# Two kinds of sums of a hybrid streaming encoder, moved from VectorE and GpSimd into accumulating transfers

## The chip, the cores and the metric

The kernel runs on one core of one Trainium2 chip. The metric is the device time of one execution in microseconds; of several runs the median counts. The engines are TensorE (PE in the profile, PEld for its weight loads), VectorE (DVE), ScalarE (ACT), GpSimd (POOL) and SyncE (SP). SP computes nothing here; it issues nearly all transfers, in order. A DMA issued by SP, ScalarE or GpSimd stands in that engine's own instruction stream.

## The reference

Two layers over 2048 tokens of width 1024. The first is a pooling mixer; the second, whose last part the change touches, is attention with 16 heads of 64 channels, followed by a gate, an output projection and a gated embedding:

```python
k_sh = rms_norm(split_heads(k_all), k_norm)
v_sh = split_heads(v_all)
q, z = jnp.split(rms_norm(x, b_norm[j]) @ b_w_in[j], 2, axis=-1)
q = rms_norm(split_heads(q), b_q_norm[j])
o = stick_breaking_attention(q, k_sh, v_sh)       # A[t,s] = beta[t,s] * prod_{s<j<t} (1 - beta[t,j])
x = x + (o * jax.nn.silu(z)) @ b_w_out[j]
x = x + (p[i] @ ple_w[i]) * jax.nn.sigmoid(x @ ple_gate_w[i])
```

The attention weight of key s for query t is the sigmoid of their logit times the product of (1 - sigmoid) over all keys between s and t. Keys after the query count nothing.

## The kernel before, in words

The first half of the program (to about 1333 us) computes the mixer layer and k, v and q, in four passes over 512 tokens each. It leaves x in DRAM (x2d, and x2p split into two parts for matmul), k, q and differences of neighbouring v rows (kd, qd, vd), and weights that are already split (wzd for z, wod for the output projection, wgd for the gate, wld for the embedding). Each fp32 operand of a matmul is held as a pair of fp32r tiles, a rounded part and the rest; a product is three matmuls, in the attention two.

The second half is attention. Four query chunks c of 512 tokens are done in the order 3, 2, 1, 0; in each, 16 heads; for each head the key chunks kc from c down to 0. One (chunk, head, key chunk) is four slots, and the loop over `n` does one slot a turn. In a slot:

- `front` (L924, L925): two matmuls make the logits of 128 queries by 512 keys, ScalarE makes 1 - sigmoid (L928, into one of four kap tiles), VectorE runs the product along the keys as a scan (L936; L933 on the diagonal chunk, where widths are 128 to 512).
- `turn`, six slots later: four transposes on TensorE (L949) into a psa bank (two of them), ScalarE copies it (L952) and VectorE makes the rest (L953), which frees the bank.
- `gather`, eight slots later: two matmuls (L961, L962) add at times v into pso.

When a head's last gather is done, pso holds 128 rows by 512 queries: 64 channels from v's rounded part, and the same 64 from the rest. ScalarE copies one half of the rows to `ob` (L976) and the other to `os` (L977), one and two slots later; two heads share an `os` and an `ob`, 64 rows each. When both heads of a pair are done, `os` and `ob` are added on VectorE (L979), which completes both heads' outputs, and `gated` follows: SP loads z's gate (L969), ScalarE adds a bias in four pieces (L972), GpSimd multiplies (L974). Later `pair_up` splits `os` into an og pair (L1006 ScalarE, L1007 GpSimd). What happens so many slots later is put off with `soon(k, fn)` and run by `settle`.

Between these, in each slot, TensorE gets filler matmuls: in chunk 3 the products for z's gate (`gate_z`, L1028 to L1034), in chunk 2 what is left of those and `post(3)`, in chunk 1 `post(2)`, in chunk 0 `post(1)`; `post(0)` is the tail. The tables `share` and `even` set how many filler matmuls a slot gets, with `stops` as the slots in which a chunk's outputs are complete.

`post(c)` has two phases over eight blocks o of 128 channels. First the output projection: weights wod (L212, by `stored`), x2d loaded into `xr` (L1065), 24 matmuls, VectorE adds the product to `xr` (L1068), and `halves` splits `xr` into an x3 pair (L1072 ScalarE, L1073 GpSimd). Then the gate and embedding: 24 matmuls for the gate and 6 for the embedding, a sigmoid into `sg` (L1092), VectorE multiplies (L1106), and the final sum adds both parts of x3 to `sg`: one on GpSimd (L1107), one on VectorE (L1108). SP stores `sg` to the output (L1112), one block late (`late`). The tiles `xr`, `sg`, `zr` and `sgz` share four buffers.

A scheduler orders the instructions of each engine by its own estimates, except those held with `keep_in_program_order` (`stay`, `held`); L972, L976, L977 and the casts are held so. Each engine works through its list in order, and an instruction that waits holds up all that stand behind it.

## Time and profile before

| what | us |
|---|---|
| median of 3 runs (2697.16 to 2699.16) | 2697.47 |
| the profiled execution | 2696.51 |
| its span, first to last instruction | 2694.7 |
| attention, chunk 3 (about) | 1333 to 1840 |
| attention, chunk 2 (about) | 1840 to 2190 |
| attention, chunk 1 (about) | 2190 to 2440 |
| attention, chunk 0 (about) | 2440 to 2596 |
| tail, `post(0)` | 2596 to 2695 |

In a row of groups stand the line, the engine, the operation, output and inputs, shape and count, then busy us, the mean ns of one, and the engine's idle time just before them with what ended it. A row of waits says who waited, for whom, for how long in all, how often, and the longest. A row of the timeline has the start, the duration, the engine and the instruction; SPq and ACTq are the issue of a transfer; the time in brackets is what the engine idled before it and what ended that. PEld rows are weight loads, and the load of a transpose is that of its moved tile.

### The profile page before, as it was taken

The numbers are of one execution on the slowest core, as the hardware profiler recorded it, in microseconds if no ns is written. First come the engines' busy times: TensorE is split into PE (matmuls) and PEld (weight loads), VectorE is DVE, ScalarE is ACT, GpSimd is POOL, SyncE is SP. The second block draws the span as 40 slices with busy tenths as digits, with TensorE's granted clock in tenths as the row PEclk, the third lists the DMA queues.
The fourth block names the chain that finished last, engine by engine and source line by source line (L and its number), as shares of the span: only waits on it lengthen the run. The fifth ranks groups of instructions, "written<-read, shape, count | busy, mean of one in ns | idle before, by whom it ended". The sixth has DMA issues, their size and how long they took to land. (4 is left out here: it accounts for less than half of the span.)

```text
span 2694.7 us, 38618 instructions
## 1 busy us (share of the span) xinstructions
PE 2673.6 (99%) x13352; PEld 2226.5 (83%) x13352; DVE 1941.9 (72%) x2506; ACT 1399.0 (52%) x2735; POOL 922.0 (34%) x724
## 2 busy tenths in 40 slices
PE   9999999999999999999999999999999999999999
PEld 8888888888888888888878888888888888888887
DVE  6776626755367643755399999999999998986632
ACT  6445523555135541445366666666666666665531
POOL 2675338643485434753121111122111211222220
PEclk9999999999999999999999999999999999999999
DMA  8657785567856678444788665555655576668865
GB/s 328 222 168 279 252 302 193 198 229 254 300 180 223 242 241 305 145 150 149 223 239 281 195 210 173 163 165 181 198 164 173 173 214 199 197 198 262 268 226 172
DMA packets 276688, 581.56 MB, mean 216 GB/s; under 512 B 33126, under 2 KB 67174, under 8 KB 276492
## 3 DMA queue, kind: packets, MB, share of 16 engines
q1 hardware_dynamic: 270754, 571.41, 64.5%
q10 hardware_dynamic: 5738, 7.68, 1.0%
q8 instruction: 106, 1.74, 0.3%
q14 instruction: 90, 0.74, 0.1%
HBM read 438.40 MB, written 132.19 MB: 212 GB/s over the span
## 5 line engine op out<-in xcount | busy, mean ns | idle before, releaser
L952 ACT CAST at<-psa 128x512 fp32r<-128x512 f32 (+3 forms) x640 | 334.3, 522 | 439.1 <-PE psa L949 429.4
L614 PE MATMUL psd<-wpair,x 128*128 128x512 f32 x2304 | 536.8, 391 | 0.0
L936 DVE TENSOR_TENSOR_SCAN pp<-kap,pp,zeros 128x512 f32<-128x512 f32 x384 | 513.1, 1336 | 6.1 <-ACT kap L928 5.1
L614 PEld LDWEIGHTS psd<-wpair,x 128*128 128x128 f32 x2304 | 429.8, 188 | 87.1
L953 DVE TENSOR_TENSOR at<-psa,at 128x512 fp32r<-128x512 f32 (+3 forms) x640 | 381.3, 596 | 82.0 <-ACT at L952 77.3
L949 PE MATMUL psa<-ident,pp 128*128 128x128 f32 x2176 | 344.6, 273 | 10.7 <-DVE at L953 10.3
L928 ACT ACTIVATE kap<-psl 128x512 f32<-128x512 f32 (+3 forms) x640 | 345.0, 539 | 13.2 <-PE psl L925 10.3
L949 PEld LDWEIGHTS psa<-ident,pp 128*128 128x128 f32 x2176 | 265.4, 140 | 77.7 <-DVE at L953 21.9
L924 PE MATMUL psl<-kk,qa 128*128 128x512 f32 (+3 forms) x640 | 282.3, 441 | 0.1
L962 PE MATMUL pso<-at,vv 128*128 128x512 f32 (+3 forms) x640 | 234.4, 366 | 1.3 <-DVE at L953 1.3
L925 PE MATMUL psl<-kk,qb 128*128 128x512 f32 (+3 forms) x640 | 232.9, 364 | 0.0
L961 PE MATMUL pso<-at,vv 128*128 128x512 f32 (+3 forms) x640 | 232.8, 364 | 0.1
L933 DVE TENSOR_TENSOR_SCAN pp<-kap,ahead 128x128 f32<-128x128 f32 (+3 forms) x256 | 227.0, 887 | 5.1 <-ACT kap L928 3.2
L167 PE MATMUL psd<-xp,wpair 128*128 128x512 f32 x512 | 199.5, 390 | 1.7 <-DVE xp L316 1.7
L166 PE MATMUL psd<-xp,wpair 128*128 128x512 f32 x512 | 200.0, 391 | 0.4 <-ACT xp L315 0.3
L168 PE MATMUL psd<-xp,wpair 128*128 128x512 f32 x512 | 199.3, 390 | 0.0
L149 DVE SCALAR_TENSOR_TENSOR wpair<-wraw,gains,wpair 128x512 fp32r<-128x512 f32 x192 | 161.4, 883 | 48.9 <-ACT wpair L148 48.9
L143 POOL TENSOR_TENSOR wpair<-wraw,wpair 128x512 fp32r<-128x512 f32 x99 | 144.0, 1464 | 84.2 <-ACT wpair L141 78.8
L148 ACT ACTIVATE wpair<-wraw,gains 128x512 fp32r<-128x512 f32 x192 | 132.7, 718 | 68.9 <-DMA wraw<-in_bq_dram 31.1
L1033 POOL TENSOR_TENSOR zr<-zr,sgz 128x512 f32<-128x512 f32 x32 | 62.0, 1938 | 307.1 <-ACT sgz L1032 269.2
L141 ACT CAST wpair<-wraw 128x512 fp32r<-128x512 f32 x148 | 89.9, 618 | 122.1 <-PE psd L168 98.9
L962 PEld LDWEIGHTS pso<-at,vv 128*128 128x128 f32 x640 | 120.3, 188 | 27.7 <-DVE at L953 1.7
(200 smaller groups left out, 5365.7 us busy)
## 6 DMA issues: line engine op xcount, KB each, us to landing
kk<-kd SPq DMA_DIRECT2D x320, 128.0 KB
vv<-vd SPq DMA_DIRECT2D x160, 256.0 KB
wraw<-in_kv_dram SPq DMA_DIRECT2D x128, 256.0 KB
wpair<-wzd SPq DMA_DIRECT2D x64, 512.0 KB
wpair<-wod SPq DMA_DIRECT2D x64, 512.0 KB
wpair<-wgd SPq DMA_DIRECT2D x64, 512.0 KB
wpair<-wu SPq DMA_DIRECT2D x48, 512.0 KB
wpair<-wi SPq DMA_DIRECT2D x36, 512.0 KB
```

Source lines behind the costliest of these rows:

```text
L166: T.matmul(ps, wst(units, kt, 0, c0), acts[kt][:, 0], start=(begin and kt == order[0]), stop=False)
L614: T.matmul(pss2[i], ck["x2"][kt][:, xh, tk], wst(ws, kt, wh, 0, W5), start=(kt == 0 and xh == 0 and wh == 0), stop=(kt == KT - 1 and wh == 1))
L924: T.matmul(ps[:, :w], qa[:, qs], kk[:, :w], start=True, stop=False)
L925: T.matmul(ps[:, :w], qb[:, qs], kk[:, :w], start=False, stop=True)
L928: A.activation(out=kp[:, r0:], in_=ps[:, :w], func=AF.Sigmoid, scale=-1.0)
L933: V.tensor_tensor_scan(out=pp[:, r0:][:, ::-1], data0=kp[:, r0:][:, ::-1], data1=ahead[:, r0:][:, ::-1], initial=1.0, op0=ALU.mult, op1=AL ...
L936: V.tensor_tensor_scan(out=pp[:, ::-1], data0=kp[:, ::-1], data1=zeros.to_broadcast([P, W5]), initial=st["carry"][j], op0=ALU.mult, op1=AL ...
L949: T.transpose(pt[:, j * P : (j + 1) * P], pp[:, r0 + kt * P : r0 + (kt + 1) * P], ident)
L952: A.copy(out=at[:, 0, cs], in_=pt[:, cs])
L953: V.tensor_tensor(out=at[:, 1, cs], in0=pt[:, cs], in1=f(at[:, 0, cs]), op=ALU.subtract)
L961: T.matmul(po[:, cs], vv[:, kt, :], at[:, 0, cs], start=(st["diag"] and kt == 0), stop=False)
L962: T.matmul(po[:, cs], vv[:, kt, :], at[:, 1, cs], start=False, stop=(st["last"] and kt == 3))
```

## The change

- In chunks 3, 2 and 1 the sum of two heads' outputs is no longer made by VectorE (L979) but by a transfer that GpSimd issues, from `ob` onto `os`, with addition. `gated` comes six slots after the last gather in place of four, and `os` is handed on after eight in place of six. Chunk 0 keeps the sum on VectorE.
- In `post(3)` and `post(2)`, `xr` (x after the output projection) is stored to the output by SP as soon as it is made. The two final sums (L1107, L1108) are gone there; in their place a transfer issued by GpSimd adds `sg` to what stands in the output, one block late as the store was. `post(1)` and `post(0)` keep the sums.
- The tables of filler matmuls count two slots more at a chunk's end.

```diff
@@ gather
                 if half:
-                    soon(3, lambda: V.tensor_tensor(out=os, in0=os, in1=ob, op=ALU.add))
-                    soon(4, gated)
-                    soon(6, lambda: outs[c].append(os))
+                    if c:
+                        soon(3, lambda: nc.gpsimd.dma_start(out=os, in_=ob, accum_op=ALU.add))
+                        soon(6, gated)
+                        soon(8, lambda: outs[c].append(os))
+                    else:
+                        soon(3, lambda: V.tensor_tensor(out=os, in0=os, in1=ob, op=ALU.add))
+                        soon(4, gated)
+                        soon(6, lambda: outs[c].append(os))
@@ post, first phase
                 V.tensor_tensor(out=xr, in0=ps, in1=xr, op=ALU.add)
                 pr = pair("x3")
+
+                if c > 1:
+                    nc.sync.dma_start(out=outt[o * P : (o + 1) * P, c * W5 : (c + 1) * W5], in_=xr)
@@ post, second phase
                 V.tensor_tensor(out=sg, in0=pl, in1=sg, op=ALU.mult)
-                (V if tail[0] else G).tensor_tensor(out=sg, in0=sg, in1=f(x3[o][:, 1]), op=ALU.add)
-                summed = soon(2, lambda o=o, sg=sg: V.tensor_tensor(out=sg, in0=sg, in1=f(x3[o][:, 0]), op=ALU.add))
-
-                def finish(o=o, sg=sg, summed=summed):
+                whole = outt[o * P : (o + 1) * P, c * W5 : (c + 1) * W5]
+                summed = lambda: None
+                if c < 2:
+                    (V if tail[0] else G).tensor_tensor(out=sg, in0=sg, in1=f(x3[o][:, 1]), op=ALU.add)
+                    summed = soon(2, lambda o=o, sg=sg: V.tensor_tensor(out=sg, in0=sg, in1=f(x3[o][:, 0]), op=ALU.add))
+
+                def finish(sg=sg, summed=summed, whole=whole):
                     summed()
-                    nc.sync.dma_start(out=outt[o * P : (o + 1) * P, c * W5 : (c + 1) * W5], in_=sg)
+                    if c > 1:
+                        nc.gpsimd.dma_start(out=whole, in_=sg, accum_op=ALU.add)
+                    else:
+                        nc.sync.dma_start(out=whole, in_=sg)
@@ the tables
-            stops[c] = 4 * (n + 1) + LAG_G + 6
+            stops[c] = 4 * (n + 1) + LAG_G + 8
-                        even = POST / (64.0 * c - (LAG_G + 2 if c == 1 else 1))
+                        even = POST / (64.0 * c - (LAG_G + 4 if c == 1 else 1))
```

Three places show how instructions move. Lines from 976 on have other numbers in the changed kernel: the transfer onto `os` is L980, the store of `xr` L1077, the transfer onto the output L1124; L1007, L1065 and L1073 of before are L1012, L1070 and L1081.

First ScalarE, at the second head pair of chunk 3, from the copy into `os` to the bias. Before:

```order
L977 COPY os<-pso 64x512
L952 CAST at<-psa 128x512
L928 ACTIVATE kap_12444<-psl 128x512
L952 CAST at<-psa 128x512
L928 ACTIVATE kap_12445<-psl 128x512
L972 ACTIVATE os<-os,en 128x128 x4
```

With the change:

```order
L977 COPY os<-pso 64x512
L952 CAST at<-psa 128x512
L928 ACTIVATE kap_12444<-psl 128x512
L952 CAST at<-psa 128x512
L928 ACTIVATE kap_12445<-psl 128x512
L952 CAST at<-psa 128x512
L928 ACTIVATE kap_12442<-psl 128x512
L1037 ACTIVATE sgz<-zr 128x512
L952 CAST at<-psa 128x512
L928 ACTIVATE kap_12443<-psl 128x512
L972 ACTIVATE os<-os,en 128x128 x4
```

The bias stands two slots further back: four copies and four sigmoids lie between, where there were two of each.

Second GpSimd, in chunk 2, where the second phase of `post(3)` begins. Before:

```order
L1007 TENSOR_TENSOR og<-os,og 128x512
L1107 TENSOR_TENSOR sg<-sg,x_19137 128x512
L974 TENSOR_TENSOR os<-os,zt 128x512
L1107 TENSOR_TENSOR sg<-sg,x_19313 128x512
L1007 TENSOR_TENSOR og<-os,og 128x512 x2
L1107 TENSOR_TENSOR sg<-sg,x_19509 128x512
```

With the change:

```order
L1012 TENSOR_TENSOR og<-os,og 128x512
L1124 DMA out_dram<-sg 128x512
L980 DMA os<-ob 128x512
L974 TENSOR_TENSOR os<-os,zt 128x512
L1012 TENSOR_TENSOR og<-os,og 128x512
L1124 DMA out_dram<-sg 128x512
```

The sums are gone, and issues of both kinds stand between the operations that stay.

Third SP, in the first phase of `post(3)`, with the change:

```order
L192 DMA qa<-qd_2_210 64x512 x2
L193 DMA qb<-qd_2_210 64x512
L1077 DMA out_dram<-xr 128x512
L193 DMA qb<-qd_2_210 64x512
L212 DMA wpair<-wod_275 128x1024
L1070 DMA xr<-x2d_4_132 128x512
L200 DMA kk<-kd_2_242 64x512 x2
```

And before, in its second phase, where the final sums are stored:

```order
L192 DMA qa<-qd_7_215 64x512
L193 DMA qb<-qd_7_215 64x512
L1112 DMA out_dram<-sg 128x512
L200 DMA kk<-kd_7_247 64x512 x2
L205 DMA vv<-vd_1_261 128x512
L212 DMA wpair<-wgd_286 128x1024
```

A store that waits for VectorE stands between loads of q, k, v and weights in both; it has moved from the second phase to the first.

## The prediction

> **What bounds the kernel now.** I read the page first, then the busy times of the four attention stages, then what TensorE waited for in them.
>
> ```profile
> span 2694.7 us, 38618 instructions
> PE 2673.6 (99%) x13352; PEld 2226.5 (83%) x13352; DVE 1941.9 (72%) x2506; ACT 1399.0 (52%) x2735; POOL 922.0 (34%) x724
> ```
>
> TensorE is busy for nearly the whole span. The change touches attention alone, so the share that matters is that of its stages. The next rows are the windows view: chunk 3, chunk 2, chunk 1, chunk 0, each with the busy time of PE, PEld, DVE, ACT and POOL, then clock, DMA share and GB/s.
>
> ```profile
> 1333.00:1840.00 507.00, 503.67 (x2776) 419.58 (x2776) 488.58 (x582) 324.94 (x650) 86.18 (x48) 1.00 0.66 203
> 1840.00:2190.00 350.00, 346.11 (x1919) 289.57 (x1918) 340.44 (x414) 230.72 (x476) 62.89 (x36) 1.00 0.57 178
> 2190.00:2440.00 250.00, 245.79 (x1359) 206.70 (x1358) 221.97 (x290) 158.40 (x348) 48.66 (x33) 1.00 0.69 206
> 2440.00:2596.00 156.00, 154.66 (x804) 129.84 (x803) 93.68 (x146) 81.71 (x195) 40.78 (x31) 1.00 0.83 254
> ```
>
> VectorE is as full as TensorE in chunks 3 and 2 (488.58 of 507, 340.44 of 350), less in chunk 1 (221.97 of 250), and has room in chunk 0. The change takes work from VectorE, and only what TensorE loses by waiting for VectorE can come back. The waits view says how much that is; the first two rows are of the window 1333 to 1840, the other two of 1840 to 2440 (total, times, longest).
>
> ```profile
> PEld psa L949 <- DVE at L953: 7.5, 15, 1.6
> PE psa L949 <- DVE at L953: 2.2, 4, 1.2
> ...
> PEld psa L949 <- DVE at L953: 14.4, 21, 1.5
> PE psa L949 <- DVE at L953: 8.1, 13, 1.1
> ```
>
> The two rows of a pair are one stall seen twice: the weight load of a transpose can't start until VectorE has emptied the bank, and the matmul behind it starts late. The matmul's row is too small (its predecessor is still drawn as busy), the load's too large (some of it is ordinary slack). So TensorE loses 8.1 to 14.4 us in chunks 2 and 1, and 2.2 to 7.5 in chunk 3. That is the ceiling of this change: 10.3 to 21.9 us, under 1% of the span. One stall in the timeline shows its origin:
>
> ```profile
> 2102.44 0.66 DVE L1106 TENSOR_TENSOR sg<-psd,sg 128x512 f32<-128x512 f32 x1
> 2103.23 1.30 POOL L1107 TENSOR_TENSOR sg<-sg,x 128x512 f32<-128x512 f32 x1 [3.62 <-PE pso L962]
> 2103.62 1.99 DVE L933 TENSOR_TENSOR_SCAN pp<-kap,ahead 128x512 f32<-128x512 f32 x1
> 2104.50 2.22 POOL L1007 TENSOR_TENSOR og<-os,og 128x512 fp32r<-128x512 f32 x1
> 2105.54 1.72 DVE L1108 TENSOR_TENSOR sg<-sg,x 128x512 f32<-128x512 f32 x1
> 2107.19 0.68 DVE L953 TENSOR_TENSOR at<-psa,at 128x512 fp32r<-128x512 f32 x1
> 2107.92 0.42 PEld L949 LDWEIGHTS psa<-ident,pp 128*128 128x128 f32 x4 [1.32 <-DVE at L953]
> ```
>
> The final sum has three steps: L1106, L1107 on GpSimd, L1108. GpSimd's step makes the scan wait (1.99 us), the next GpSimd operation makes L1108 wait (1.72), L953 comes late, and the transposes start 1.32 us late. So a final sum costs VectorE more than its own instruction.
>
> **The change, part by part.** First what goes. The rows are of the grouped lines, window 1333 to 1840 and then 1840 to 2440 (busy, mean ns):
>
> ```profile
> L979 DVE TENSOR_TENSOR os<-os,ob 128x512 f32<-128x512 f32 x8 | 5.3, 665 | 0.0
> ...
> L979 DVE TENSOR_TENSOR os<-os,ob 128x512 f32<-128x512 f32 x16 | 11.8, 736 | 0.0
> L1107 POOL TENSOR_TENSOR sg<-sg,x 128x512 f32<-128x512 f32 x16 | 22.6, 1414 | 86.6 <-DVE sg L1106 62.1 <-PE psl L925 20.9 <-PE pso L962 3.6
> L1108 DVE TENSOR_TENSOR sg<-sg,x 128x512 f32<-128x512 f32 x15 | 18.5, 1236 | 6.4 <-POOL sg L1107 6.4
> ```
>
> VectorE loses 5.3 us in chunk 3 (1% of its 488.58) and 11.8 + 18.5 = 30.3 in chunks 2 and 1 (5% of 562.4; the 16th final sum lies just past the window). GpSimd loses 22.6 us of operations that also block the scans. What that gives TensorE lies between 0, if the stalls stay for other reasons, and the ceiling. In chunks 2 and 1 I take three quarters of the middle of 8.1 and 14.4, so 8.5 us: the stalls cluster at the final sums, while L1007 and L1073 on GpSimd remain and still collide with scans. In chunk 3 only 1% of VectorE's work goes and no final sum; there I take 1 us of 2.2 to 7.5. Gross gain 9.5.
>
> **The wait that is added.** The four activations L972 add a bias to os, in ScalarE's fixed order, and must now wait until the accumulating transfer has landed. Behind them on ScalarE stand the copies L952, which free the transposes' banks, and the sigmoids L928, which feed the scans; so a late transfer would stop all three engines. The time it has:
>
> ```profile
> 1414.22 0.67 DVE L979 TENSOR_TENSOR os<-os,ob 128x512 f32<-128x512 f32 x1
> ...
> 1472.01 0.58 ACT L977 COPY os<-pso 64x512 f32<-64x512 f32 x1
> ...
> 1473.22 0.67 DVE L979 TENSOR_TENSOR os<-os,ob 128x512 f32<-128x512 f32 x1
> ...
> 1475.68 1.27 ACT L972 ACTIVATE os<-os,en 128x128 f32<-128x128 f32 x4
> ...
> 1479.09 0.60 ACT L928 ACTIVATE kap<-psl 128x512 f32<-128x512 f32 x1
> ```
>
> Two head pairs are 59.0 us or 32 slots apart, 1.84 us a slot. Today L972 follows L977 by 3.7 us. By the order of the change it comes two slots later, behind the L928 that ran from 1479.09 to 1479.69. The transfer can start when L977 ends, at 1472.59, so it has 7.1 us. No transfer from GpSimd and none that accumulates is in this trace. The nearest rows are copies within SBUF with a GpSimd operation waiting for them, one in attention, one from the dense stage:
>
> ```profile
> 1354.75 0.54 SPq L670 DMA_DIRECT2D vl<-vl  x1
> 1358.00 1.45 POOL L690 TENSOR_TENSOR vl<-vl 128x512 f32<-128x512 f32 x1 [3.10 <-DMA vl<-vl]
> ...
> 329.58 1.86 ACTq L668 DMA_DIRECT2D vs<-vr  x2
> 337.70 1.29 POOL L690 TENSOR_TENSOR vs<-vs,vr 128x512 f32<-128x512 f32 x1 [6.57 <-DMA xn<-in_x_dram]
> ```
>
> The first took at most 3.3 us from issue to use, the second up to 8.1. I take 4.5, nearer the row from attention, since the accumulation reads two operands. To it comes the time until GpSimd issues: 0 if it is idle (it is busy 86.18 of 507 us in chunk 3), up to the 2.22 of L1007 above; I take 1.3. Sum 5.8 us, inside 7.1, cost 0. The far ends, 8.1 + 2.22 = 10.3, would be 3.2 us late. How much of a delay ScalarE swallows is shown by its idle time at the copies (all of attention):
>
> ```profile
> L952 ACT CAST at<-psa 128x512 fp32r<-128x512 f32 x448 | 262.8, 587 | 305.7 <-PE psa L949 302.9 <-PE psl L924 2.5
> ```
>
> 305.7 us over 448 slots is 0.7 us a slot. So a transfer late by x costs about x − 0.7 for each of the 24 head pairs: at most 2.5 x 24 = 60 us.
>
> **GpSimd's issues.** Forty instructions on GpSimd are new, 24 for os and 16 for the output. The longest block above is the scan of 1.99 us; the same scan with no GpSimd operation beside it:
>
> ```profile
> 2058.85 1.22 DVE L933 TENSOR_TENSOR_SCAN pp<-kap,ahead 128x512 f32<-128x512 f32 x1
> ```
>
> If each issue blocks a scan as L1107 did, for 1.99 − 1.22 = 0.77 us, that is 40 x 0.77 = 31 us of VectorE, nearly what was taken away; if none does, 0. Since 35.6 us of VectorE bought 9.5 here, 31 would give back 8.3. I take somewhat under a third, 2.5, because the issue neither reads nor adds 128x512 elements. The Trainium skill, page "SBUF — State Buffer", section "Who interferes with whom", says that a VectorE operation with two SBUF inputs contends only with a GpSimd operation that reads SBUF; by that rule the term would be 0 and the sum 2.5 us lower. The trace agrees as far as it goes (GpSimd's sums read SBUF and block); it has no issue to show.
>
> **SP's queue.** Sixteen stores of xr are added and the sixteen final stores of these chunks leave. Both wait at the head of the queue for VectorE, with kk, vv and weight loads behind them:
>
> ```profile
> SPq L1112 <- DVE sg L1108: 32.1, 11, 5.1
> SPq L1065 <- POOL x L1073: 24.4, 8, 6.2
> ```
>
> (SP's waits, window 1840 to 2440.) Today's blocks of up to 5.1 and 6.2 us delay no matmul, since the loads run ahead; like replaces like, so 0. If that cover were gone, 16 blocks of 32.1 / 11 = 2.9 us would cost 47 us, but nothing points to it. An xr buffer is now also held by its store, beside L1073, which already holds it for a conversion and a GpSimd sum; 0. The table of slots shifts by two; TensorE's work stays the same; 0.
>
> **Sum.** −8.5 − 1 + 2.5 = −7. The profiled execution took 2696.51 us (span 2694.7 and 1.8 around it), the median of the runs is 2697.47, 1 us more; so 2690.5 us. Less than 0.2% (5.4 us) can't be told from no change in this kernel.
>
> **Rivals.** *The transfer lands late* (slower). One mechanism: L972 waits on ScalarE. It decides from 7.8 us (7.1 + 0.7) between L977's end and landing. With the dense row's 8.1 and the issue's 1.3, it is 9.4: 1.6 x 24 = 38, less the gain of 7, +31 us, 2728; with half that excess (8.6 us) 19 − 7 = +12, 2709. For it: VectorE is full, GpSimd and it have been seen to hold each other up, and the weight loads share the DMA engines (0.57 to 0.69 busy). Against it: the attention row, 3.3. A rule of the skill belongs here. The same page, section "SBUF: two separate sides", says that VectorE in its two-port mode keeps GpSimd from writing descriptors, and gives 620 ns that grew to 3100. If scans did that, my 5.8 would grow by 2.5, an estimate from that page, to 8.3 and cost 0.5 x 24 = 12 us, the sum +5. The page ties it to copies and casts and not to scans, and no row here has such a mode beside an issue. Chance 0.2, price 2702 to 2728.
>
> *TensorE is the bound anyway* (no change). TensorE shows 346.11 busy of 350 in chunk 2; if L1007, L1073 and the new issues cause the stalls that L1107 and L1108 cause now, the gain is 0 to 4 us: 2693.5 to 2699. For it: L1007 stands beside L1107 in the stall shown. Against it: that stall needed both. Chance 0.27.
>
> *All of the waits go*: the ceiling's middle, 16 us, 2681. It would need chunk 3's waits to go as well, where only 1% of VectorE's load does. Chance 0.05.
>
> **How the numbers follow.** Forecast 0.48, with its own range 2685 to 2694. Its upper edge lies within 0.2% of before (2692.1): of its 0.48 about 0.07 counts as the same. Faster 0.41 + 0.05 = 0.46; same 0.07 + 0.27 = 0.34; slower 0.2. The range from 2682 to 2711 leaves out the far half of the late transfer (0.1) and most of the last rival, 2 in 10 with the tails.
>
> **What would show it.** Right: L949's waits for L953 in 1840 to 2440 fall to a third; scans of about 2 us become rare; ScalarE shows no wait of L972 for a DMA; SP's wait at the new store is like L1112's. Wrong: a row of L972 waiting for os over 0.7 us a time (late transfer), waits at L949 that stay and are ended by scans that an issue made long, or psl matmuls that wait for kk loads behind the store of xr. The prediction is wrong in its sign if accumulation or the issue on GpSimd takes longer than the 7.1 us allow, since I have no row of it.

## The result, and the profile after

The changed kernel takes 2691.72 us (median of 10 runs, 2689.05 to 2692.76), before takes 2697.22 (10 runs, 2695.92 to 2699.16). The ratio is 0.9978, 95% interval 0.9969 to 0.9987: 5.5 us faster, just over the 0.2% that this kernel's measurement can tell. The profiled execution took 2690.62 us.

The page, its first two rows that answer to those of before:

```profile
span 2688.5 us, 38660 instructions
...
PE 2671.2 (99%) x13352; PEld 2228.4 (83%) x13352; DVE 1906.4 (71%) x2466; ACT 1400.6 (52%) x2735; POOL 927.6 (35%) x748
```

VectorE lost 35.5 us and 40 instructions, TensorE has the same 13352 matmuls, and the span is 6.2 us shorter. The windows view of chunk 3, chunk 2, chunk 1 and chunk 0 (columns as before; the last window now ends at 2590):

```profile
1333.00:1840.00 507.00, 504.16 (x2785) 421.47 (x2784) 485.75 (x575) 327.02 (x653) 90.07 (x56) 1.00 0.68 207
1840.00:2190.00 350.00, 349.89 (x1948) 294.72 (x1947) 328.90 (x408) 235.47 (x485) 64.62 (x47) 1.00 0.66 195
2190.00:2440.00 250.00, 247.03 (x1361) 208.48 (x1360) 208.30 (x276) 159.44 (x352) 50.52 (x41) 0.99 0.82 225
2440.00:2590.00 150.00, 148.66 (x771) 124.92 (x770) 87.02 (x134) 76.12 (x180) 39.03 (x29) 1.00 0.80 253
```

The same stretches hold more matmuls in chunks 3 and 2. The waits view says why; the first two rows are of the window 1333 to 1840, the other four of 1840 to 2440 (total, times, longest):

```profile
PEld psa L949 <- DVE at L953: 4.0, 5, 1.0
PE psa L949 <- DVE at L953: 1.9, 5, 0.5
...
ACT os L972 <- DMA os<-ob: 4.5, 4, 2.6
PEld psa L949 <- DVE at L953: 2.9, 5, 1.3
ACT ob L976 <- DMA os<-ob: 2.3, 1, 2.3
...
PE psa L949 <- DVE at L953: 1.3, 3, 0.9
```

In chunks 2 and 1 TensorE's wait for VectorE fell from 8.1 and 14.4 us (the two views of one stall) to 1.3 and 2.9. Two rows are new. L972 waits for the accumulating transfer, 4.5 us in four cases. And L976, the copy into `ob`, waits for it once, 2.3 us.

Where the time went is clearest by chunk. The table gives each stretch from the end of one chunk's last copy L977 to the end of the next's (chunk 3 from the end of its first head's copy), worked out from the trace. "Loss" is what the stretch takes beyond its matmuls, where each matmul counts with the median distance from one of its shape to the next.

| | chunk 3 | chunk 2 | chunk 1 | chunk 0 | tail |
|---|---|---|---|---|---|
| before, us | 442.9 | 355.5 | 251.0 | 160.3 | 101.4 |
| after, us | 440.2 | 350.1 | 246.6 | 165.3 | 101.7 |
| before, loss | 11.4 | 11.7 | 9.7 | 5.5 | 5.6 |
| after, loss | 9.7 | 6.7 | 5.6 | 8.9 | 5.9 |

The loss fell by 10.8 us in the first three chunks and grew by 3.4 in chunk 0. That chunk is 5.0 us longer because 1.6 us of filler matmuls also moved into it (837 matmuls in place of 830). Ahead of attention, where nothing was changed, this profile is 1.0 us longer, and the tail 0.3. So −10.8 + 3.4 + 1.3 = −6.1, the span's −6.2.

A single profile scatters. Two kernels below differ from the change only at the end of chunk 1, and their chunk 3 loses about 11 us where the change's loses 9.7. So of a difference in one chunk's loss, about 1 us can be chance.

Chunk 0's loss has one place. The timeline of the change at the end of chunk 1:

```profile
2420.93 0.58 ACT L977 COPY os<-pso 64x512 f32<-64x512 f32 x1
...
2421.82 0.86 POOL L980 DMA_DIRECT2D os<-ob  x1 [4.71 <-ACT os L977]
...
2428.53 0.58 ACT L976 COPY ob<-pso 64x512 f32<-64x512 f32 x1 [2.25 <-DMA os<-ob]
2429.30 0.39 ACT L928 ACTIVATE kap<-psl 128x256 f32<-128x256 f32 x1
2429.57 1.27 ACT L972 ACTIVATE os<-os,en 128x128 f32<-128x128 f32 x4
2430.74 0.57 ACT L977 COPY os<-pso 64x512 f32<-64x512 f32 x1
2432.17 0.49 ACT L928 ACTIVATE kap<-psl 128x384 f32<-128x384 f32 x1
2432.71 0.33 PE L924 MATMUL psl<-kk,qa 128*128 128x128 f32 x1 [1.48 <-ACT kap L928]
```

There is one `ob` tile. A head of chunk 0 has a single key chunk, four slots, so its copy into `ob` comes soon after the last pair of chunk 1, while that pair's transfer still reads the tile. ScalarE stands 2.25 us, the sigmoids L928 behind it come late, and the logits' matmul L924 starts 1.48 us late (1.65 by the matmuls' starts). The windows around it show a second loss:

```profile
2430.00:2434.00 4.00, 2.29 (x16) 1.91 (x15) 2.57 (x5) 3.79 (x11) 2.13 (x2) 1.00 0.47 119
2434.00:2438.00 4.00, 4.00 (x14) 3.19 (x13) 3.73 (x6) 2.48 (x8) 1.77 (x1) 0.58 1.06 250
```

After the stall the granted clock falls to 0.58 in these 4 us: TensorE does 14 matmuls while it looks fully busy.

### The profile page after: what moved, and what is told of

The parts are those of the page before. It is cut to its first block, busy times and chain, and to the rows that moved or that the text cites. A ratio compares the mean times of both kernels' runs of the same rounds, so it can differ in the third digit from the quotient of the medians.

```text
span 2688.5 us, 38660 instructions
## 1 busy us (share of the span) xinstructions
PE 2671.2 (99%) x13352; PEld 2228.4 (83%) x13352; DVE 1906.4 (71%) x2466; ACT 1400.6 (52%) x2735; POOL 927.6 (35%) x748
## 5 line engine op out<-in xcount | busy, mean ns | idle before, releaser
L952 ACT CAST at<-psa 128x512 fp32r<-128x512 f32 (+3 forms) x640 | 334.5, 523 | 426.7 <-PE psa L949 411.7
L936 DVE TENSOR_TENSOR_SCAN pp<-kap,pp,zeros 128x512 f32<-128x512 f32 x384 | 511.1, 1331 | 4.9 <-ACT kap L928 3.8
L928 ACT ACTIVATE kap<-psl 128x512 f32<-128x512 f32 (+3 forms) x640 | 344.7, 539 | 13.2 <-PE psl L925 10.4
L949 PE MATMUL psa<-ident,pp 128*128 128x128 f32 x2176 | 343.9, 273 | 3.5 <-DVE at L953 3.2
L949 PEld LDWEIGHTS psa<-ident,pp 128*128 128x128 f32 x2176 | 267.0, 140 | 65.6 <-DVE at L953 6.9
L924 PE MATMUL psl<-kk,qa 128*128 128x512 f32 (+3 forms) x640 | 282.3, 441 | 1.8 <-ACT kap L928 1.5
L933 DVE TENSOR_TENSOR_SCAN pp<-kap,ahead 128x128 f32<-128x128 f32 (+3 forms) x256 | 220.1, 860 | 7.1 <-ACT kap L928 4.9
```

The source lines that it names most:

```text
L924: T.matmul(ps[:, :w], qa[:, qs], kk[:, :w], start=True, stop=False)
L928: A.activation(out=kp[:, r0:], in_=ps[:, :w], func=AF.Sigmoid, scale=-1.0)
L933: V.tensor_tensor_scan(out=pp[:, r0:][:, ::-1], data0=kp[:, r0:][:, ::-1], data1=ahead[:, r0:][:, ::-1], initial=1.0, op0=ALU.mult, op1=AL ...
L936: V.tensor_tensor_scan(out=pp[:, ::-1], data0=kp[:, ::-1], data1=zeros.to_broadcast([P, W5]), initial=st["carry"][j], op0=ALU.mult, op1=AL ...
L949: T.transpose(pt[:, j * P : (j + 1) * P], pp[:, r0 + kt * P : r0 + (kt + 1) * P], ident)
L952: A.copy(out=at[:, 0, cs], in_=pt[:, cs])
```

## The experiments

Kernels that ran together share their runs of before, and each ratio stands against that median. These medians lie between 2697.08 and 2698.26, so a difference between two rows with other runs of before is uncertain by about 1 us.

| kernel | median us (range) | before | ratio, 95% |
|---|---|---|---|
| last pair of chunk 1 on VectorE | 2687.77 (2685.76 to 2688.80) | 2698.26 | 0.9960, 0.9946 to 0.9973 |
| last pair's transfer in four | 2691.08 (2687.65 to 2694.45) | 2697.35 | 0.9977, 0.9969 to 0.9986 |
| final sums alone | 2689.55 (2689.07 to 2691.43) | 2698.26 | 0.9969, 0.9956 to 0.9981 |
| sums of two heads alone | 2697.00 (2694.45 to 2702.45) | 2698.26 | 0.9998, 0.9989 to 1.0007 |
| bias as early as before | 2724.87 (2723.38 to 2728.06) | 2698.26 | 1.0100, 1.0086 to 1.0114 |
| final transfers in quarters | 2687.89 (2687.20 to 2689.32) | 2697.22 | 0.9966, 0.9953 to 0.9978 |
| shift alone | 2700.57 (2698.33 to 2702.74) | 2697.22 | 1.0013, 1.0004 to 1.0022 |
| final sums and shift | 2692.01 (2690.28 to 2693.88) | 2697.35 | 0.9981, 0.9972 to 0.9990 |
| the same, tables as before | 2689.49 (2688.43 to 2690.13) | 2697.08 | 0.9972, 0.9960 to 0.9983 |
| last pair on VectorE, bias one slot later | 2689.72 (2688.18 to 2690.58) | 2697.22 | 0.9972, 0.9961 to 0.9983 |
| os transfers in chunks 3 and 2 only | 2686.62 (2685.94 to 2688.53) | 2697.22 | 0.9961, 0.9949 to 0.9974 |
| the same, tables as before | 2689.12 (2688.63 to 2689.96) | 2697.08 | 0.9970, 0.9959 to 0.9982 |

### Is it the single ob tile that costs chunk 0 its time?

```diff
-                        soon(3, lambda: nc.gpsimd.dma_start(out=os, in_=ob, accum_op=ALU.add))
+                        if c > 1 or h2 < 7:
+                            soon(3, lambda: nc.gpsimd.dma_start(out=os, in_=ob, accum_op=ALU.add))
+                        else:
+                            soon(3, lambda: V.tensor_tensor(out=os, in0=os, in1=ob, op=ALU.add))
```

> The change, with one edit: the last head pair of chunk 1 is summed by VectorE again (its bias stays two slots later). Theory A: the 5.1 us that chunk 0 lost (end of chunk 1 to end of chunk 0: 160.3 us before, 165.4 after) come from the single ob tile. Chunk 0's first head has one key chunk, so its copy into ob comes four slots after the last copy of chunk 1, while the transfer still reads ob; ScalarE stands 2.25 us, TensorE 1.6 us, and its clock then falls to half for 3.4 us. If so the half clock after the boundary is gone and the time falls by 3 to 3.5 us, to 2688 to 2689. Rival B: chunk 0 lost time to the later tables (filler work moved past the boundary), which this edit keeps; then the time stays at 2691 to 2692.

Measured 2687.77: 3.9 us faster than the change, and every run is below every run of it. The same place in its timeline:

```profile
2422.25 0.69 DVE L983 TENSOR_TENSOR os<-os,ob 128x512 f32<-128x512 f32 x1
...
2426.69 0.58 ACT L976 COPY ob<-pso 64x512 f32<-64x512 f32 x1
```

and the same two windows:

```profile
2430.00:2434.00 4.00, 3.77 (x22) 3.17 (x21) 3.38 (x5) 3.77 (x10) 2.23 (x3) 1.00 0.75 196
2434.00:2438.00 4.00, 4.00 (x23) 3.39 (x22) 2.59 (x6) 2.56 (x8) 1.74 (x2) 1.00 0.89 206
```

L976 no longer waits for anything, TensorE does 22 and 23 matmuls where it did 16 and 14, and the clock stays at 1.00. Chunk 0 takes 161.8 us in place of 165.3, a loss of 5.3 as in before (5.5). Theory A holds, and the 1.5 us that remain over before's 160.3 are the filler matmuls that moved.

The opposite test, a longer hold of `ob`:

```diff
-                        soon(3, lambda: nc.gpsimd.dma_start(out=os, in_=ob, accum_op=ALU.add))
+                        soon(3, lambda: [nc.gpsimd.dma_start(out=os[e], in_=ob[e], accum_op=ALU.add)
+                                         for e in ([slice(r, r + 32) for r in range(0, P, 32)]
+                                                   if (c, h2) == (1, 7) else [slice(0, P)])])
```

> The change, with the last pair's transfer of chunk 1 in four transfers of 32 rows each, issued one behind the other: ob stays occupied for the three further issues of about 0.9 us less the shorter landing (4.2 us for a quarter, 5.5 for the whole), so 1.4 to 2 us longer. Theory A (the copy L976 of chunk 0's first head waits for ob, TensorE stands, and the clock may fall to half): L976's wait grows from 2.3 to about 4 us, TensorE's stall from 1.6 to 3 to 3.5 us, and the half clock follows in nearly every run: 2693.5 to 2695.5. Rival B (chunk 0 loses for another reason): no difference to the change, 2691 to 2692.

Measured 2691.08, as the change. This doesn't speak against theory A, since the edit didn't do what it was to do. The four transfers wait by rows: those of the first head went out a head earlier, and only two were left at the end. Its timeline:

```profile
2406.28 1.63 POOL L980 DMA_DIRECT2D os<-ob  x2 [5.28 <-ACT os L977]
...
2421.72 1.58 POOL L980 DMA_DIRECT2D os<-ob  x2 [4.69 <-ACT os L977]
...
2428.04 0.58 ACT L976 COPY ob<-pso 64x512 f32<-64x512 f32 x1 [2.17 <-DMA os<-ob]
```

and its two windows:

```profile
2430.00:2434.00 4.00, 2.29 (x14) 1.83 (x13) 2.65 (x5) 3.79 (x11) 2.15 (x2) 1.00 0.56 127
2434.00:2438.00 4.00, 4.00 (x21) 3.28 (x20) 3.24 (x5) 2.65 (x8) 1.79 (x1) 1.00 1.03 241
```

L976 waits 2.17 us (2.25 in the change), and TensorE stands 1.64 us (1.65). So the dose was not raised; half of the bytes took nearly as long to land (5.9 and 5.5 us for the two transfers, 6.7 for the whole in the change). But the profile is worth having: the same stall, and here the clock stays at 1.00 afterwards, with 21 matmuls where the change did 14. Chunk 0 takes 163.3 us against 165.3: the half clock is 2.0 us (1.7 by the clock row, (1 − 0.58) x 4), the stall itself the other 1.5 (163.3 − 161.8). It may also be what spreads the runs of both kernels (by 3.7 and 6.8 us). The other runs left no trace, but the mean granted clock of each is on record. Of the change's ten runs eight are at 0.999 or below (mean 2691.8 us) and two at 1.000 (2689.8); of this kernel's eleven, seven are at 0.999 (2692.1) and four at 1.000 (2689.5). Where in those runs the clock fell isn't shown.

### The two halves of the change

Only the sums of two heads by transfer (final sums and their single store as before):

```diff
-                if c > 1:
-                    nc.sync.dma_start(out=outt[o * P : (o + 1) * P, c * W5 : (c + 1) * W5], in_=xr)
...
-                        nc.gpsimd.dma_start(out=whole, in_=sg, accum_op=ALU.add)
+                (V if tail[0] else G).tensor_tensor(out=sg, in0=sg, in1=f(x3[o][:, 1]), op=ALU.add)
+                summed = soon(2, lambda o=o, sg=sg: V.tensor_tensor(out=sg, in0=sg, in1=f(x3[o][:, 0]), op=ALU.add))
```

> Only half of the change: the sums of two heads by transfer (with bias and tables two slots later); the final sums and the one store per block as before. By the forecast's terms (1 us gross gain in chunk 3; os sums are 4 of VectorE's 30 us in chunks 2 and 1, so 1.1 of 8.5; 24 of 40 issues): 2.1 - 1.5 = 0.6 us faster than before, 2696.5. The boundary loss (theory A) stays in it: with it about 3 us slower than before, 2700. Rival: the os sums matter as much as the final sums, because each stands between a scan and an L953: 5 us faster.

Only the final sums by transfer (sums of two heads, bias and tables as before):

```diff
-                        soon(3, lambda: nc.gpsimd.dma_start(out=os, in_=ob, accum_op=ALU.add))
-                        soon(6, gated)
-                        soon(8, lambda: outs[c].append(os))
+                    soon(3, lambda: V.tensor_tensor(out=os, in0=os, in1=ob, op=ALU.add))
+                    soon(4, gated)
+                    soon(6, lambda: outs[c].append(os))
...
+            stops[c] = 4 * (n + 1) + LAG_G + 6
```

> The other half: the final sums of query chunks 3 and 2 by transfer, with the store of xr; the sums of two heads on VectorE with the bias and the tables as before. By the forecast's terms 7.4 - 1 = 6.4 us faster than before; by what the traces show (9.8 us of gross gain in chunks 2 and 1, most of it from these sums, and no loss at the boundary since ob is free) 8 to 9 us, 2688 to 2689.5: faster than the whole change. Rival: both halves are needed for the stalls to go, as each leaves a sum between scans; then 3 to 4 us faster, 2694.

The final sums alone are worth 8.7 us, more than the whole change. The sums of two heads, with the shift, are 1.3 us faster, with an interval from 3.0 faster to 1.9 slower: not to be told from nothing. The eleven runs of that kernel spread by 8.0 us, from 2694.45 at a granted clock of 1.000 to 2702.45 at 0.997, and its profile (2694.70) is of one of the fastest. The waits of L949 in 1840 to 2440, first of the kernel with only the sums of two heads by transfer:

```profile
PEld psa L949 <- DVE at L953: 9.8, 15, 2.4
PE psa L949 <- DVE at L953: 5.2, 7, 2.1
```

and of the kernel with only the final sums by transfer:

```profile
PEld psa L949 <- DVE at L953: 4.9, 9, 0.9
PE psa L949 <- DVE at L953: 1.7, 6, 0.4
```

Before had 14.4 and 8.1, the change has 2.9 and 1.3. So the final sums, with GpSimd's step between VectorE's two, carried most of the stalls. Which of the three steps did it isn't tested. In the profile of the first half, chunk 0 lost 2.3 us more than before, but the longest stall there, 1.87 us, is ended by a load of q, and L976 waits only 1.0 us for the transfer; the boundary of chunks 1 and 0 has more than one way to go wrong.

### Was the late bias needed, and does the price of a late transfer hold?

```diff
-                        soon(6, gated)
-                        soon(8, lambda: outs[c].append(os))
+                        soon(4, gated)
+                        soon(6, lambda: outs[c].append(os))
...
-            stops[c] = 4 * (n + 1) + LAG_G + 8
+            stops[c] = 4 * (n + 1) + LAG_G + 6
```

> The change with the bias four slots after the last gather as before (in place of six) and the old tables: L972 on ScalarE comes 3.7 us after the copy L977, while in the profile of the change the transfer has landed 3.6 to 9.2 us after it (median about 5.9). The prediction's price for a transfer late by x is (x - 0.7) x 24: with x = 2.2 this is 36 us less the fast ones, so 25 to 35 us slower than the change, 2717 to 2727. Rival: TensorE has filler matmuls and ScalarE's idle time swallows nearly all of it: 5 us or less slower.

Measured 2724.87: 33.2 us over the change and 26.6 over before. This is the late transfer of the prediction's rival, and its size is near what the price said. The waits in attention:

```profile
ACT os L972 <- DMA os<-ob: 52.2, 23, 6.0
PEld psa L949 <- DVE at L953: 40.1, 45, 4.5
```

52.2 / 23 is 2.27 us a pair; (2.27 − 0.7) x 24 = 37.7 by the price, 33.2 by the runs. Two things in this trace aren't in the price. The waits differ by chunk: 17.9 us for the pairs of chunk 3, 5.6 for those of chunk 2, and 28.7 for those of chunk 1; the losses of chunks 3 and 1 grow by about 14 us each and that of chunk 2 by 2.4. And TensorE's granted clock is 0.79 in 1424 to 1432, 0.83 in 2392 to 2402 and 0.76 in 2456 to 2470, together 6.7 us of time where the change lost 1.7. So about 5 of the 33.2 us are half clock. The tables are those of before as well. One of the waits, in the timeline:

```profile
1423.58 1.28 ACT L972 ACTIVATE os<-os,en 128x128 f32<-128x128 f32 x4 [5.91 <-DMA os<-ob]
1424.77 0.56 ACT L952 CAST at<-psa 128x512 fp32r<-128x512 f32 x1
...
1425.36 0.69 DVE L953 TENSOR_TENSOR at<-psa,at 128x512 fp32r<-128x512 f32 x1 [6.27 <-ACT at L952]
...
1426.11 0.66 PE L949 MATMUL psa<-ident,pp 128*128 128x128 f32 x4 [4.09 <-DVE at L953]
```

This is the chain that the prediction described: the bias stands, the copy L952 behind it is late, VectorE runs dry, TensorE's bank isn't freed. The shift of two slots is what saves the change from it.

### What does an issue on GpSimd cost?

The kernel with only the final sums by transfer, with 64 issues in place of 16:

```diff
-                        nc.gpsimd.dma_start(out=whole, in_=sg, accum_op=ALU.add)
+                        for e in range(4):
+                            nc.gpsimd.dma_start(out=whole[e * 32 : (e + 1) * 32], in_=sg[e * 32 : (e + 1) * 32], accum_op=ALU.add)
```

> The kernel with only the final sums by transfer, each of the 16 transfers split into four of 32 rows: 48 more issues on GpSimd, at 0.87 us each 42 us more of its queue. Nobody waits soon for these transfers, so it measures the issue alone. By the prediction's term (2.5 us for 40 issues) 3 us slower than that kernel, 2692.5; by its upper bound (0.77 us of VectorE each, 9.5 us of time for 35.6 of VectorE) 10 us slower, 2699.5; if an issue blocks no scan (in the change 18 scans beside an issue took 1.28 us, as without one) no difference, 2689.5.

Measured 2687.89, not slower than the 2689.55 with 16 issues. The groups of 1840 to 2440 (busy, mean ns), first of the kernel with 16, then with 64:

```profile
L936 DVE TENSOR_TENSOR_SCAN pp<-kap,pp,zeros 128x512 f32<-128x512 f32 x184 | 243.3, 1322 | 3.6 <-ACT kap L928 2.9
...
L1119 POOL DMA_DIRECT2D out_dram<-sg x16 | 14.2, 887 | 88.9 <-PE psa L949 38.5 <-ACT kap L928 24.5 <-DVE sg L1109 17.8
```

```profile
L936 DVE TENSOR_TENSOR_SCAN pp<-kap,pp,zeros 128x512 f32<-128x512 f32 x184 | 244.5, 1329 | 3.2 <-ACT kap L928 2.6
...
L1120 POOL DMA_DIRECT2D out_dram<-sg x64 | 54.6, 1178 | 80.0 <-DVE sg L1109 45.7 <-PE psa L949 34.2
```

GpSimd issues for 40 us more and the scans take 1.2 us more in 184 (1329 against 1322 ns). In the change, 18 scans L936 that ran beside an issue and no other GpSimd operation took 1277 ns, those beside nothing 1275, and 115 beside a GpSimd operation 1462 on average. An issue costs the scans nothing that these runs show. The Trainium skill, page "SBUF — State Buffer", section "Who interferes with whom", has it so: a VectorE operation with two SBUF inputs contends with a GpSimd operation that reads SBUF, and not with one that only writes it. The trace agrees with its 1277, 1275 and 1462 ns, as far as an issue isn't such a read; what an issue reads isn't shown.

### Is the shift free?

Only the bias, hand-over and tables two slots later, all sums as before:

```diff
-                        soon(3, lambda: nc.gpsimd.dma_start(out=os, in_=ob, accum_op=ALU.add))
+                        soon(3, lambda: V.tensor_tensor(out=os, in0=os, in1=ob, op=ALU.add))
                         soon(6, gated)
                         soon(8, lambda: outs[c].append(os))
```

(The final sums and the store are those of before too.)

> Only the shift: all sums on VectorE and GpSimd and one store per block as before, but the bias six slots after the last gather, the hand-over after eight, and the tables two slots later, as in the change. The prediction put the shift at 0. If so: no difference to before (2698), with chunk 0 about 1.5 us longer (161.8 in place of 160.3) and the chunks ahead of it shorter by as much, since filler work only moves. Rival B: the later hand-over itself loses 2 to 4 us at the chunks' ends, 2700 to 2702.

Measured 2700.57: 3.35 us slower than before, interval 1.1 to 5.9. The profiled execution, 2698.33, was the fastest of the eleven, so its profile holds only 1.8 us of this (span 2696.5 against 2694.7). Chunk 0 is 1.5 us longer as expected, but chunks 3 and 2 didn't get shorter; their losses grew from 11.4 and 11.7 to 12.7 and 12.6. New stalls of 1.5 and 2.2 us stand at the boundary of chunks 2 and 1, behind the final sums. I took this for their cause:

```diff
+                    soon(6 if c else 4, gated)
+                    soon(8 if c else 6, lambda: outs[c].append(os))
...
+            stops[c] = 4 * (n + 1) + LAG_G + 8
...
+                        even = POST / (64.0 * c - (LAG_G + 4 if c == 1 else 1))
```

(Edit to the kernel with only the final sums by transfer.)

> Final sums by transfer (with the store of xr), sums of two heads on VectorE, but bias, hand-over and tables two slots later as in the change. The shift alone cost about 3 us while the final sums were still made by GpSimd and VectorE. Theory C: the cost is theirs: with the shift L1112 on GpSimd and L1113 fall behind the scan at the boundary of chunks 2 and 1, where TensorE stands 1.5 and 2.2 us. Without these sums the shift then costs nothing, 2689.5 as without it (2689 to 2691). Rival D: the later hand-over itself costs the 3 us, 2692 to 2693, and the change carries it too.

Measured 2692.01, 2.5 us more than without the shift. Theory C falls: the final sums are gone here and the cost is about as large, at other places. In its profile the loss is spread: 0.9 us more in chunk 3, 0.4 less in chunk 2, 0.4 more in chunk 1, 1.0 in chunk 0, where the first head's load of k lands late:

```profile
2429.79 0.30 PE L924 MATMUL psl<-kk,qa 128*128 128x128 f32 x1 [0.90 <-DMA kk<-kd]
```

The next two runs ask which part of the shift it is. First this kernel with the tables of before:

```diff
-            stops[c] = 4 * (n + 1) + LAG_G + 8
+            stops[c] = 4 * (n + 1) + LAG_G + 6
...
-                        even = POST / (64.0 * c - (LAG_G + 4 if c == 1 else 1))
+                        even = POST / (64.0 * c - (LAG_G + 2 if c == 1 else 1))
```

> Final sums by transfer, sums of two heads on VectorE, bias and hand-over two slots later as in the change, but the tables of filler matmuls as before. The shift as a whole cost 2.5 us here (2692.0 against 2689.55). If the tables carry that cost (seven filler matmuls, 1.6 us of TensorE's work, come in chunk 0 in place of chunk 3, and each slot's mix changes), 2689.5; if the later bias and hand-over carry it, 2692.

Measured 2689.49, the 2689.55 of the kernel without any shift. So here the tables carry the cost, and a later bias and hand-over are free to about 1 us. In the two profiles 1.9 of the 2.3 us of loss lie in chunk 0 (6.5 against 4.6); whether `stops` or `even` did it isn't tested. What the tables do beside transfers of os is asked by the last run of the next group.

### A version that beats both, and the tables once more

Transfers of os in chunks 3 and 2 alone, chunk 1 with VectorE and its old distances:

```diff
-                    if c:
+                    if c > 1:
                         soon(3, lambda: nc.gpsimd.dma_start(out=os, in_=ob, accum_op=ALU.add))
...
+            stops[c] = 4 * (n + 1) + LAG_G + (8 if c > 1 else 6)
...
+                        even = POST / (64.0 * c - (LAG_G + 2 if c == 1 else 1))
```

> Final sums by transfer, sums of two heads by transfer in chunks 3 and 2 alone; chunk 1 sums on VectorE with the bias four slots after the last gather, tables there as before. If the parts add (chunk 3 gained 2.5 us and chunk 2 1.8 us from the os transfers, chunk 1 5.1 us from the final sums, and chunk 0 loses nothing when no transfer holds ob at its start): 4.3 us faster than the final sums alone, 2685 to 2686. Rival: chunk 1's own os transfers are worth the 1.5 us that the trace shows there, and this equals the kernel with only the last pair on VectorE, 2687.8.

Measured 2686.62, 5.1 us faster than the change, all runs below all of it; the losses are 10.6, 6.7, 5.1 and 5.2 us. It lies between the two expectations (2685 to 2686, 2687.8) and its range overlaps with that of the kernel with only the last pair on VectorE, so these runs don't tell what chunk 1's own transfers of os are worth. With `stops` as before too, so that all tables are:

```diff
-            stops[c] = 4 * (n + 1) + LAG_G + (8 if c > 1 else 6)
+            stops[c] = 4 * (n + 1) + LAG_G + 6
```

> Final sums by transfer, sums of two heads by transfer in chunks 3 and 2 with bias and hand-over two slots later, chunk 1 on VectorE; all tables of filler matmuls as before. The same kernel with the tables of chunks 3 and 2 two slots later took 2686.6. If the tables carry the shift's cost, 1 to 2.5 us faster, 2684 to 2685.5; if not, 2686.6, or more if filler matmuls now wait for outputs that come two slots later than the tables count on.

Measured 2689.12, 2.5 us slower, with no run in common. So later tables cost 2.5 us in one kernel and gain 2.5 in another. The two edits aren't the same, though: here `stops` alone differs, while the pair above also differs in `even`, which sets chunk 0's rate, and lost mainly in chunk 0. In the profiles 0.9 us of the gain is chunk 3's loss (11.5 against 10.6), no more than profiles of the same work scatter. But a stall of 1.35 us at the end of chunk 3 (at 1780.5 in before, 1781.9 here) stands in every profile with the old `stops` and in none with the later ones. Still, the shifted tables lost elsewhere in the kernels that they made slower, and 1.2 us of this profile lie ahead of attention, so the cause of the sign stays open. What is shown is the size: how the filler matmuls fall among the slots is worth 2.5 us either way, nearly half of what the whole change gained.

The last try, with the bias one slot later still:

```diff
-                        soon(6, gated)
-                        soon(8, lambda: outs[c].append(os))
+                        soon(7, gated)
+                        soon(9, lambda: outs[c].append(os))
...
+            stops[c] = 4 * (n + 1) + LAG_G + 9
```

(Edit to the kernel with the last pair on VectorE.)

> The kernel with the last pair of chunk 1 on VectorE, and the bias seven slots after the last gather in place of six (8.9 us after L977 in place of 7.1), the hand-over after nine, the tables three slots later. There the bias still waits 3.6 us for transfers in chunk 1. If these waits reach TensorE, 1 to 2 us faster than that kernel (2686 to 2687); if ScalarE's idle time swallows them, as with the prediction's 0.7 us a slot, no difference (2687.8).

Measured 2689.72, about 2 us slower than that kernel: a miss for both expectations. L972's waits for transfers are gone from its profile, and the time didn't fall. That doesn't show that ScalarE's idle time had swallowed them, since the tables moved once more: chunk 1, where the waits were, loses 4.2 us in place of 5.6, chunk 2 loses 7.3 in place of 6.5, and chunk 0 has 0.9 us more of filler work and a new stall of 1.47 us behind a late load of k.

## Why the prediction was right, and where it wasn't

The forecast was 2690.5 us, measured 2691.72: right in sign and in its main mechanism, VectorE's stalls. That the size is so close is partly luck: two of its terms were wrong, and it missed one.

**The ceiling and the gross gain** hold. Taken were 8.5 us in chunks 2 and 1 and 1 us in chunk 3, 9.5 in all; the losses fell by 9.1 and 1.7, 10.8 in all (the 1.7 would be about 0.4 by the two other profiles whose chunk 3 is the same work). The waits of L949 in 1840 to 2440 fell to a fifth or less, where a third was forecast; three quarters of the ceiling's middle was somewhat low. Scans over 1.8 us among the 128x512 ones of this window went from 7 of 216 to 3 of 217. The rival that L1007 and L1073 would keep the stalls alive is refuted. The split by the same terms was right in direction: 6.4 us for the final sums against 8.7 measured, and 0.6 for the others, whose 1.3 can't be told from nothing.

**The added wait at L972** shows no cost to TensorE, as forecast, but the margin was thinner. The prediction's own signs were off here: it expected no such wait, and called a wait of over 0.7 us a time the sign of the late transfer. The waits are 4.5 us in four cases, 1.1 each, and the change is still faster. The one stall of TensorE over 0.7 us in chunk 1, 1.11 us at 2298, stands as 1.10 in the kernel whose chunk 1 has no transfer of os. The transfers, in the list of issues (KB each, median us from issue to landing):

```profile
os<-ob POOLq DMA_DIRECT2D x24, 256.0 KB, 5.6
...
out_dram<-sg POOLq DMA_DIRECT2D x16, 256.0 KB, 4.9
```

The landing takes 5.6 us where 4.5 was taken, the wait for GpSimd before it 0.3 where it was 1.3; the sum of 5.9 hits the forecast's 5.8 by luck. Single ones land after 3.3 to 8.4 us, and one figure for all 24 was too coarse: the median is 4.7 us in chunk 3, 4.3 in chunk 2 and 6.7 in chunk 1, where the DMA share is highest too (0.68, 0.66 and 0.82). Of L972's 4.5 us of waits 4.3 are in chunk 1. The price (x − 0.7) x 24 came near with the earlier bias (37.7 by the price, 33.2 measured, of which about 5 are half clock), so the rival of the late transfer was a real one, two slots away.

**GpSimd's issues**, 2.5 us, were mis-sized: they cost nothing. The bound from L1107's block (0.77 us each) was the wrong neighbour: GpSimd's sums lengthen a scan beside them (1462 ns) and the issues don't (1277). The rule of the Trainium skill named beside the term (page "SBUF — State Buffer", section "Who interferes with whom") gave 0, as measured.

**SP's queue** cost nothing, as forecast, though the wait moved: the new store waits little, and z's load L969 waits more, behind a slower path to its only buffer (window 1840 to 2440):

```profile
SPq L969 <- POOL os L974: 44.4, 13, 6.9
...
SPq L1077 <- DVE xr L1073: 10.8, 14, 1.6
```

In the change no stalled matmul named it. In three of the other kernels a load of k or q did end a stall at the boundary of chunks 1 and 0 (0.9 to 1.9 us), so this cover isn't certain. The new store also holds its buffer: x's load L1070 waits for it, 10.6 us in four cases, where the prediction saw no wait; no matmul shows it.

**The step that failed** is "The wait that is added". It followed the transfer to its consumer, L972, and not to the tile that it reads. The sum on VectorE left `ob` 0.7 us after it began; the transfer holds it for some 6. Between pairs there is room, but not at the boundary of chunks 1 and 0. That costs 3.4 us of loss in the profile and 3.9 in the medians.

**The shift of the tables**, put at 0 because TensorE's work stays the same, is the other wrong term. The whole shift cost 3.35 us by itself and 2.5 beside the final sums by transfer, and the later `stops` gained 2.5 beside transfers of os; what it is worth in the change itself wasn't measured. The sum came out right by luck: the gross gain was 1.3 higher and the issues 2.5 lower than taken, which nearly pays for `ob`.

## What to carry to other kernels

When a computation becomes a transfer, follow both ends: who waits for the result, and who wants to overwrite the source, above all where a loop gets shorter. Move to transfers those sums whose engine steps block each other, not all that can be moved: here the final sums alone gave 8.7 us, and the fastest kernel measured left chunk 1's pairs on VectorE. Where the order of fillers is set by a table, a change of two slots is worth some 2 to 3 us here by itself, so hold the table fixed or measure it apart before giving a few microseconds to a cause.

## What the runs showed of the hardware that was not expected

- A TensorE stall of 1.65 us was followed by about 3.4 us at half clock ((1 − 0.58) x 4 / 0.5), 1.7 us of time; the same stall of 1.64 us in another kernel was not. The Trainium skill, page "TensorE: Matmul & The Clock Gate", section "What's actually happening", gives an idle window of about 3.4 us as the condition. Here TensorE wasn't idle so long: it was busy for 2.29 of the 4 us before. The page also says that the window runs freely. The traces agree: each keeps the times at which the clock changed, and those times inside one trace lie whole multiples of 3.413 us apart. In the kernel with the bias as early as before, the clock falls at 1426.667, 2396.052 and 2460.905 us, 284.0 and 19.0 such steps apart. In the change the step just ahead of the fall, 2431.25 to 2434.66, has TensorE busy for 1.71 of 3.41 us. In the other kernel the same stall falls into two steps, busy for 2.65 and 2.47. So where a stall lies in these steps may decide. The busy time alone doesn't: with only the shift, a step with 1.53 (2195.71 to 2199.12) was followed by no fall.
- An accumulating transfer of 256 KB took 3.3 to 8.4 us from issue to landing. Onto the output, one of 64 KB had a median of 4.2 us and the whole of 256 KB 5.4: a quarter of the bytes took over three quarters of the time.
- Its issue occupies GpSimd for 0.87 to 0.89 us, and VectorE's scans don't notice.
